# Tying modulation matmuls to the first of their group, and making the first layer's shifts and scales in halves, in a four-layer transformer kernel

## The chip, the cores and the metric

The kernel runs on one core of a Trainium2 chip. The metric is the device time of one execution in microseconds (us), the median of several runs. TensorE does matrix products, VectorE and ScalarE elementwise work (ScalarE also copies and activations), GpSimd a little of it, SyncE (SP) issues the transfers between main memory (HBM) and the on-chip memory. Each engine executes its own queue of instructions in order; semaphores join the queues.

## The reference

256 latent and 256 context tokens of 2048 features go through four blocks: windowed attention with sinks, latent attention (MLA), an RWKV layer with a pooling branch, and full attention. What matters here is the modulation of each block and its use, for two condition vectors (latent and context):

```python
cond = jax.nn.silu(c)[:, None, :]
...
shift, scale, gate = jnp.split(cond @ ada_w[i] + ada_b[i], 3, axis=-1)
h = rmsnorm(x, norm_g[i]) * (1.0 + scale) + shift
...
x = x + gate * o
```

A modulation weight is 2048 by 6144: 2048 columns each for shift, scale and gate. All of it is in 32-bit floating point; the four weights together are 192 MB.

## The kernel before, in words

Feature-major activations `h` lie on chip as two tensors, a high and a low part; each large product is three matmuls (`mm3`, lines 349 to 354: high by high, low by high, high by low), and weights are split on the way in (`split`, lines 314 to 325: a cast on ScalarE at line 323, a difference on VectorE at line 324).

The modulation (`mod_steps`, lines 243 to 281) is a generator that other stages advance step by step, so that its matmuls stand between theirs. The columns are taken in 12 groups of 512: 0 to 3 shift, 4 to 7 scale, 8 to 11 gate. A group's weights come in four loads of 1 MB (`mod_load`, line 240; 192 loads for the four layers), and each load is a group of four matmuls (line 260) that write to four strips of 32 partitions of one PSUM bank, `tile_position=(0, 32 * j)`: the stationary operand has 32 columns only, of which two hold the conditions. When a batch of groups is summed up, ScalarE copies the bank out (line 267), four small matmuls with a selection matrix add the strips up and turn them (line 273), and VectorE adds the bias (line 279). For the first layer a batch is a shift group with its scale group, for the gates and in the other layers four groups.

No order is written out by hand: the program's instructions have priorities in the order in which they are traced, and a scheduler with a model of the engines picks, for each engine, what it thinks ready first. It may put other matmuls between two of one group.

The opening (`tile_network`, from line 1670) loads the activations in four tiles, sums their squares (`add_sq`: squares on ScalarE, lines 1519 and 1522, sums on VectorE, line 1523), makes the reciprocal root and spreads it over the features (lines 464, 456, 474), and then, for each of four blocks `g` of 512 features, waits for the block's shift and scale (`need`), makes the scales (lines 532 and 535) and the four feature tiles of `h` (`put_h`: line 494, cast at 498, difference at 500). Two jobs follow each block, cut into steps: `keys`, the key projection of the block's features (weight tiles `raw`, two feature tiles in each, from two buffers) and `values(g)`, the value projection of the same features into a partial sum `vp` (weight tiles `rawv`, one buffer). Modulation tiles `mraw` have three buffers in the opening. Two modulation loads are issued ahead of the activations, on SP's queue like all others.

Of the kernel before, what the change touches and what calls it, by code (L numbers as in the profile page):

```python
# [13 lines left out]
ALU = mybir.AluOpType  # L14
# [4 lines left out]
P = 128  # L19
D = 2048  # L20
KD = D // P
# [36 lines left out]
VF = 0  # L58
# [12 lines left out]
BKB = 1  # L71


MOD_BATCHES = ((0, 4), (1, 5), (2, 6), (3, 7), (8, 9, 10, 11)), ((0, 4, 1, 5), (2, 6, 3, 7), (8, 9, 10, 11))


_VECS = [
# [39 lines left out]
class Net:  # L117
# [90 lines left out]
    def modulation(self):  # L208
        self.mod = [self.pc.tile([P, 48, 2], F32, name=f"mod{i}") for i in range(4)]
        self.mod_done = set()  # L210
        order = [(i, g) for i in range(4) for gs in MOD_BATCHES[min(i, 1)] for g in gs]
        self.mod_loads = [(i, g, q) for i, g in order for q in range(4)]
        self.mod_ahead, self.mod_pool, self.mod_wait = [], None, 0
        self.side["mod"] = (self.mod_steps(), 0)

# [17 lines left out]
    def mod_load(self):  # L233

        self.mod_wait = 0
        if self.mod_pool and self.mod_loads:
            pool, bufs = self.mod_pool
            raw = pool.tile([P, 4, 512], F32, tag="mraw", name=self.nm("mraw"), bufs=bufs)
            i, g, q = self.mod_loads.pop(0)
            self.nc.sync.dma_start(out=raw, in_=self.I["mod_w"][i, g, q])  # L240
            self.mod_ahead.append(raw)

    def mod_steps(self):
        nc = self.nc
        for i in range(4):
            if i % 2 == 0:
                self.conditions(i // 2)
            mod, cs = self.mod[i], self.cs
            for gs in MOD_BATCHES[min(i, 1)]:
                pb = self.bank("mv")  # L250
                for n, g in enumerate(gs):
                    for q in range(4):
                        while len(self.mod_ahead) < (self.mod_pool[1] - 1 if self.mod_pool and self.mod_loads else 0):
                            self.mod_load()
                        if not self.mod_ahead:
                            self.mod_load()
                        raw = self.mod_ahead.pop(0)
                        for j in range(4):
                            k = 4 * q + j
                            nc.tensor.matmul(  # L260
                                pb[32 * j : 32 * j + 32, :], cs[:, 32 * k + 30 - 2 * n : 32 * k + 62 - 2 * n], raw[:, j, :],
                                start=(n == 0 and q == 0), stop=(n == len(gs) - 1 and q == 3), tile_position=(0, 32 * j),
                            )
                        self.mod_wait = MOD_LAG
                        yield
                ev = self.t512("ev")
                nc.scalar.copy(ev, pb)
                for _ in range(MV_LAG):
                    yield
                p2 = self.bank("mv2")  # L270
                c = 2 * len(gs)
                for j in range(4):
                    nc.tensor.matmul(
                        p2[:, c * j : c * j + c], ev[:, j * P : (j + 1) * P], self.sel[:, :c], start=True, stop=True
                    )
                for n, g in enumerate(gs):
                    bias = self.v("mod_b", i * 48 + g * 4, 4).unsqueeze(2).broadcast_to([P, 4, 2])
                    pv = p2[:, : 4 * c].rearrange("p (j n c) -> p j n c", j=4, c=2)[:, :, n, :]
                    nc.vector.tensor_tensor(mod[:, g * 4 : (g + 1) * 4, :], pv, bias, op=ALU.add)
                    self.mod_done.add((i, g))  # L280
                yield


# [1387 lines left out]
def tile_network(ctx, tc, I, out, dbg=None, stop=9):  # L1671
    N = Net(ctx, tc, I, out, dbg)
    nc = N.nc
# [3 lines left out]
    mod, h = N.mod, N.h  # L1677


    pv = ctx.enter_context(ExitStack())  # L1680
    pV = pv.enter_context(tc.tile_pool(name="v0", bufs=1))
    vh, vl = [pV.tile([P, 4, 512], F32R, name=n) for n in ("vhswa", "vlswa")]
    with tc.tile_pool(name="x0", bufs=1) as px:
        x = [px.tile([P, 4, NT], F32, tag="x0", name=N.nm("x0"), bufs=4) for _ in range(4)]
        acc = px.tile([P, NT], F32, name="acc0")
        N.mod_open(px, 3, 0)
        N.mod_load()
        N.mod_load()
        for k4 in range(0, KD, 4):
            nc.sync.dma_start(out=x[k4 // 4], in_=I["x"][:, k4 : k4 + 4, :])  # L1690
            for k in range(k4, k4 + 4):
                N.add_sq(acc, k, x[k4 // 4][:, k % 4, :])
        pr = N.rms_spread(acc, 4)
        rr = px.tile([P, NT], F32, name="rr0")
        nc.scalar.copy(rr, pr)
        s0 = N.pc.tile([P, KD, 2], F32, name="s0")
        vacc = px.tile([P, 4, 512], F32, name="vacc")

        def keys(kb):

            kb.update({t: N.acc() for t in range(4)})
            for k, wh, wl in N.weights(I["swa_in"][0], KD, 512):
                for t in range(4):
                    s = slice(t * P, (t + 1) * P)
                    N.mm3(kb[t], h[0][:, k, s], h[1][:, k, s], wh, wl, k == 0, k == KD - 1)
                    yield

        def values(g):


            if g < 2:
                whi, wlo = h[0][:, 12:16, :], h[1][:, 12:16, :]
            else:
                whi, wlo = [px.tile([P, 4, 512], F32R, tag="x0", name=N.nm("vw"), bufs=4) for _ in range(2)]
            for q in range(2):
                raw = px.tile([P, 1024], F32, tag="rawv", name=N.nm("rawv"), bufs=RV)
                nc.sync.dma_start(out=raw.rearrange("p (k c) -> p k c", k=2), in_=I["swa_in"][1, 2 * g + q])
                for k in range(2):
                    N.hilo_sb(whi[:, 2 * q + k, :], wlo[:, 2 * q + k, :], raw[:, 512 * k : 512 * k + 512])
            for t in range(4):  # L1720
                s = slice(t * P, (t + 1) * P)
                pb = N.bank("vp")
                for n in range(4):
                    k = 4 * g + n
                    N.mm3(pb, h[0][:, k, s], h[1][:, k, s], whi[:, n, :], wlo[:, n, :], n == 0, n == 3)
                    if n < 3:
                        yield
                if g == 0:
                    nc.scalar.copy(vacc[:, t, :], pb)
                else:  # L1730
                    nc.vector.tensor_tensor(vacc[:, t, :], vacc[:, t, :], pb, op=ALU.add)
                if g == 3:
                    N.hilo_sb(vh[:, t, :], vl[:, t, :], vacc[:, t, :])
                yield

        kb = {}
        kgen = keys(kb)
        todo = []
        for g in range(4):
            owed = 0.0  # L1740
            while len(todo) > VK:
                next(todo.pop(0))
                owed += VR
                while owed >= 1.0:
                    owed -= 1.0
                    if not all((0, i) in N.mod_done for i in (g, 4 + g)):
                        next(N.side["mod"][0])
            N.need(0, (g, 4 + g))
            N.scales(mod[0], N.v("norm_g", 0, KD), s0, 4 * g, 4 * g + 4)
            for k in range(4 * g, 4 * g + 4):  # L1750
                t = N.t512("xr")
                nc.vector.tensor_tensor(t, x[g][:, k % 4, :], rr, op=ALU.mult)
                N.put_h(k, t, s0, mod[0][:, 0:16, :], BOTH)
            todo += [values(g)] * 16 + [kgen] * 16 if VF and g == 3 else [kgen] * 16 + [values(g)] * 16
        owed = 0.0
        while todo:
            next(todo.pop(0))
            owed += VE
            if owed >= 1.0:
                owed -= 1.0  # L1760
                N.advance("mod", 1)
        N.mod_close()
# [3 lines left out]
    with tc.tile_pool(name="x1", bufs=1) as px:  # L1766
# [7 lines left out]
        w = I["swa_out"]  # L1774
# [24 lines left out]
    with tc.tile_pool(name="x2", bufs=1) as px:  # L1799
# [4 lines left out]
        w = I["mla_out"]  # L1804
# [36 lines left out]
    with tc.tile_pool(name="x3", bufs=1) as px:  # L1841
# [4 lines left out]
        gs = N.pc.tile([P, KD, 2], F32, name="gs")  # L1846
# [9 lines left out]
        w = I["ev_out"]  # L1856
# [30 lines left out]
    with tc.tile_pool(name="x4", bufs=1) as px:  # L1887
# [10 lines left out]
        w = I["od_out"]  # L1898
# [39 lines left out]
def layout(inp):  # L1938
    inp = {k: np.asarray(v) for k, v in inp.items()}
    f32 = np.float32  # L1940
    A = {}
# [2 lines left out]
    A["x"] = tok(np.concatenate([ctx, x], axis=0))  # L1944
    A["ctx2"] = tok(inp["ctx_2"][0])
    quads = lambda w: w.reshape(4, 4, P, 12, 512).transpose(3, 0, 2, 1, 4)
    A["mod_w"] = np.ascontiguousarray(np.stack([quads(w) for w in (*inp["ada_w"], *inp["mod_w_2"])]))

    pr, pe = _pairs(P), _pairs(64)
# [10 lines left out]
    w = inp["mla_w_in"][0]  # L1960
# [3 lines left out]
    w = inp["mla_w_qb"][0].reshape(512, 16, 192)  # L1964
    A["mla_qb"] = _tiles(w[:, :, :128].reshape(512, -1), HG * P)
    A["mla_qp"] = _tiles(w[:, :, 128:][:, :, pe].reshape(512, -1), 256)
    w = inp["mla_w_kvb"][0].reshape(256, 16, 256)
# [4 lines left out]
    w = inp["ev_w_in_2"][0]  # L1972
# [22 lines left out]
    for n, g, p in (  # L1995
# [3 lines left out]
        g = inp[g][0][p]  # L1999
# [7 lines left out]
    i = np.arange(P)  # L2007
# [33 lines left out]
```

## Time and profile before

| | |
|---|---|
| median of 3 runs | 3298.6 us (3296.96 to 3299.93) |
| the profiled execution | 3288.34 us, its span 3286.3 us |
| mean granted TensorE clock | 0.983 of full speed |
| TensorE busy (matmuls) | 3117.3 us, 95% of the span, 19762 records |
| VectorE, ScalarE busy | 2101.0 us (64%), 1481.1 us (45%) |
| read from and written to HBM | 517.46 MB, 35.13 MB |

The profile was taken in one execution that was some 10 us shorter than the median of the others. Busy time is a sum over a group of instructions, with overlaps counted once; a matmul's record lasts longer than its spacing to the next, because matmuls are pipelined, so the starts of two records are the safer measure of what one costs. A matmul of the modulation has two records.

### The profile page before, as it was taken

The numbers are of one execution on the slowest core, as the hardware profiler recorded it, in microseconds if no ns is written. First come the engines' busy times: TensorE is split into PE (matmuls) and PEld (weight loads), VectorE is DVE, ScalarE is ACT, GpSimd is POOL, SyncE is SP. The second block draws the span as 40 slices with busy tenths as digits, with TensorE's granted clock in tenths as the row PEclk, the third lists the DMA queues.
The fourth block names the chain that finished last, engine by engine and source line by source line (L and its number), as shares of the span: only waits on it lengthen the run. The fifth ranks groups of instructions, "written<-read, shape, count | busy, mean of one in ns | idle before, by whom it ended". The sixth has DMA issues, their size and how long they took to land. (4 is left out here: it accounts for less than half of the span.)

```text
span 3286.3 us, 53227 instructions
## 1 busy us (share of the span) xinstructions
PE 3117.3 (95%) x19762; PEld 2397.2 (73%) x19762; DVE 2101.0 (64%) x4647; ACT 1481.1 (45%) x3233; POOL 351.2 (11%) x536
## 2 busy tenths in 40 slices
PE   5999999999988999999999999999999999899997
PEld 2567777767777788897776676666677768678897
DVE  2446454553376666666777788777787546857766
ACT  2424444442276666653334334333343323646664
POOL 0000000000001111000122222221121101200000
PEclk8999999999999999999999999999999999999999
DMA  8843444348654666766434433334434474543454
GB/s 303 309 165 135 139 137 157 125 174 290 234 165 142 226 208 226 253 228 211 126 98 133 124 125 116 111 103 149 126 109 154 168 253 130 172 140 129 143 180 153
DMA packets 270771, 556.07 MB, mean 169 GB/s; under 512 B 122928, under 2 KB 150704, under 8 KB 244912
## 3 DMA queue, kind: packets, MB, share of 16 engines
q1 hardware_dynamic: 270512, 552.68, 50.8%
q8 instruction: 155, 2.54, 0.3%
q14 instruction: 104, 0.85, 0.1%
HBM read 517.46 MB, written 35.13 MB: 168 GB/s over the span
## 5 line engine op out<-in xcount | busy, mean ns | idle before, releaser
L324 DVE TENSOR_TENSOR wlo<-raw,whi 128x512 fp32r<-128x512 f32 (+2 forms) x1000 | 660.3, 668 | 572.7 <-ACT whi L323 538.3
L352 PE MATMUL a<-hhi,whi 128*128 128x512 f32 (+1 forms) x2752 | 972.8, 355 | 16.6 <-ACT whi L323 11.9
L323 ACT CAST whi<-raw 128x512 fp32r<-128x512 f32 (+2 forms) x1000 | 593.0, 599 | 815.4 <-PE a L353 470.8
L353 PE MATMUL a<-hlo,whi 128*128 128x512 f32 (+1 forms) x2752 | 947.3, 345 | 0.0
L354 PE MATMUL a<-hhi,wlo 128*128 128x512 f32 (+1 forms) x2752 | 940.0, 347 | 4.5 <-DVE wlo L324 4.3
L352 PEld LDWEIGHTS a<-hhi,whi 128*128 128x128 f32 x2752 | 525.6, 191 | 145.2 <-issue 45.0
L354 PEld LDWEIGHTS a<-hhi,wlo 128*128 128x128 f32 x2752 | 522.6, 191 | 63.5 <-DVE wlo L324 10.2
L353 PEld LDWEIGHTS a<-hlo,whi 128*128 128x128 f32 x2752 | 526.3, 191 | 46.0 <-issue 2.2
L456 POOL TENSOR_TENSOR rs<-st,mhalf 128x4 f32<-128x4 f32 (+3 forms) x109 | 145.7, 1337 | 1683.3 <-DVE st L453 1666.3
L260 PE MATMUL mv<-mraw,cs 128*32 128x512 f32 x1536 | 258.3, 629 | 16.5 <-DMA mraw<-mod_w 16.2
L352 PE MATMUL a<-whi,hhi 128*128 128x512 f32 (+1 forms) x672 | 260.6, 398 | 13.4 <-ACT sq L613 5.9
L353 PE MATMUL a<-wlo,hhi 128*128 128x512 f32 (+1 forms) x672 | 262.7, 391 | 1.4 <-DVE wlo L324 1.1
L354 PE MATMUL a<-whi,hlo 128*128 128x512 f32 (+1 forms) x672 | 258.8, 388 | 0.0
L1427 POOL TENSOR_SCALAR SD<-SV,DL 64x64 f32<-64x64 f32 x224 | 130.0, 580 | 468.7 <-DVE SV L1438 452.4
L352 PEld LDWEIGHTS a<-whi,hhi 128*128 128x128 f32 x672 | 126.1, 190 | 71.2 <-issue 18.6
L353 PEld LDWEIGHTS a<-wlo,hhi 128*128 128x128 f32 x672 | 127.9, 190 | 31.5 <-DVE wlo L324 7.3
L354 PEld LDWEIGHTS a<-whi,hlo 128*128 128x128 f32 x672 | 127.6, 190 | 25.4 <-issue 0.8
L565 ACT ACTIVATE pr<-sc,nm 128x512 f32<-128x512 f32 (+1 forms) x128 | 81.1, 633 | 90.2 <-DVE nm L562 66.7
L1430 ACT COPY SV<-chain 64x64 f32<-64x64 f32 x128 | 26.6, 208 | 184.5 <-DVE SV L1429 178.8
L556 DVE TENSOR_REDUCE mx<-sc 128x1 f32<-128x512 f32 (+1 forms) x128 | 78.9, 617 | 37.8 <-PE sc L766 15.9
L260 PEld LDWEIGHTS mv<-mraw,cs 128*32 128x32 f32 x1536 | 37.0, 110 | 87.8 <-issue 50.3
L1444 ACT COPY y<-chain 64x64 f32<-64x64 f32 x256 | 52.9, 207 | 98.2 <-PE chain L1441 87.8
(379 smaller groups left out, 4690.6 us busy)
## 6 DMA issues: line engine op xcount, KB each, us to landing
mraw<-mod_w SPq DMA_DIRECT2D x192, 1024.0 KB, 4.9
raw<-od_in SPq DMA_DIRECT2D x88, 512.0 KB, 3.6
raw<-swa_in SPq DMA_DIRECT2D x72, 512.0 KB, 3.6
raw<-ev_rkv SPq DMA_DIRECT2D x64, 384.0 KB, 3.4
raw<-ev_in SPq DMA_DIRECT2D x48, 512.0 KB, 3.9
raw<-swa_out SPq DMA_DIRECT2D x40, 512.0 KB, 5.6
raw<-ev_out SPq DMA_DIRECT2D x40, 512.0 KB, 3.6
raw<-mla_g SPq DMA_DIRECT2D x64, 256.0 KB, 3.3
```

The lines of the kernel that those rows point to most:

```text
L260: nc.tensor.matmul(pb[32 * j : 32 * j + 32, :], cs[:, 32 * k + 30 - 2 * n : 32 * k + 62 - 2 * n], raw[:, j, :], start=(n == 0 and q == 0), ...
L323: nc.scalar.copy(whi, raw)
L324: nc.vector.tensor_tensor(wlo, raw, whi.bitcast(F32), op=ALU.subtract)
L352: mm(out, ah, bh, start=first, stop=False, skip_group_check=shared)
L353: mm(out, ah, bl, start=False, stop=False, skip_group_check=shared)
L354: mm(out, al, bh, start=False, stop=last, skip_group_check=shared)
L456: self.nc.gpsimd.tensor_tensor(dst, stv, mv, op=ALU.pow)
L556: nc.vector.reduce_max(mx, sc, axis=AX.X)
L565: nc.scalar.activation(pr[:, :n], sc, AF.Exp, scale=scale, bias=nm, accum_out=sm)
L1427: nc.gpsimd.tensor_scalar(SD[r_], SV[r_, hh, c, :], DL[r_, c : c + 1], None, ALU.mult)
L1430: nc.scalar.copy(SV[half[1], 1, c, :], ps[half[1], P : P + L])
L1444: nc.scalar.copy(y[r_, c, :], blk(3 * P, hh))
```

## The change

The first layer's shift and scale weights get a second layout, `mod_h`: 256 columns to a piece, so that a load of 1 MB holds 8 blocks of 128 rows instead of 4, and a piece takes two loads. A batch is then one half of a shift group with the same half of its scale group, and the opening goes by halves `u` of a block: two feature tiles, half the steps of `keys`, and `values` after the second half. The activations are loaded first, and three modulation loads after them instead of two before. In all layers the matmuls of a load that follow the first one get the highest priority and an edge that keeps them behind the matmul traced before them.

```diff
+MOD_FIRST = tuple(((g, u), (4 + g, u)) for g in range(4) for u in range(2)) + ((8, 9, 10, 11),)
+MOD_BATCHES = (0, 4, 1, 5), (2, 6, 3, 7), (8, 9, 10, 11)
...
     def mod_load(self):
...
-            self.nc.sync.dma_start(out=raw, in_=self.I["mod_w"][i, g, q])
+            if isinstance(g, tuple):
+                raw = raw.rearrange("p k (a c) -> p (k a) c", a=2)
+                self.nc.sync.dma_start(out=raw, in_=self.I["mod_h"][g[0], g[1], q])
+            else:
+                self.nc.sync.dma_start(out=raw, in_=self.I["mod_w"][i, g, q])
...
-            for gs in MOD_BATCHES[min(i, 1)]:
+            for gs in MOD_BATCHES if i else MOD_FIRST:
                 pb = self.bank("mv")
+                half = isinstance(gs[0], tuple)
+                nq, nk, cols = (2, 8, 256) if half else (4, 4, 512)
                 for n, g in enumerate(gs):
-                    for q in range(4):
+                    for q in range(nq):
...
-                        for j in range(4):
-                            k = 4 * q + j
-                            nc.tensor.matmul(
-                                pb[32 * j : 32 * j + 32, :], cs[:, 32 * k + 30 - 2 * n : 32 * k + 62 - 2 * n], raw[:, j, :],
-                                start=(n == 0 and q == 0), stop=(n == len(gs) - 1 and q == 3), tile_position=(0, 32 * j),
-                            )
+
+                        for kk in range(nk):
+                            k, j = nk * q + kk, kk % 4
+                            with self.tc.high_priority(None if kk else 0):
+                                mm = nc.tensor.matmul(
+                                    pb[32 * j : 32 * j + 32, :cols], cs[:, 32 * k + 30 - 2 * n : 32 * k + 62 - 2 * n],
+                                    raw[:, kk, :], start=(n == 0 and k < 4), stop=(n == len(gs) - 1 and k >= KD - 4),
+                                    tile_position=(0, 32 * j),
+                                )
+                                if kk:
+                                    self.tc.keep_in_program_order(mm)
                         self.mod_wait = MOD_LAG
                         yield
-                ev = self.t512("ev")
-                nc.scalar.copy(ev, pb)
+                ev = self.t512("ev", cols=cols)
+                nc.scalar.copy(ev, pb[:, :cols])
...
         N.mod_open(px, 3, 0)
-        N.mod_load()
-        N.mod_load()
         for k4 in range(0, KD, 4):
             nc.sync.dma_start(out=x[k4 // 4], in_=I["x"][:, k4 : k4 + 4, :])
             for k in range(k4, k4 + 4):
                 N.add_sq(acc, k, x[k4 // 4][:, k % 4, :])
+        for _ in range(3):
+            N.mod_load()
...
-        for g in range(4):
+        for g, u in ((g, u) for g in range(4) for u in range(2)):
             owed = 0.0
...
-            N.need(0, (g, 4 + g))
-            N.scales(mod[0], N.v("norm_g", 0, KD), s0, 4 * g, 4 * g + 4)
-            for k in range(4 * g, 4 * g + 4):
+            N.need(0, ((g, u), (4 + g, u)))
+            k0 = 4 * g + 2 * u
+            N.scales(mod[0], N.v("norm_g", 0, KD), s0, k0, k0 + 2)
+            for k in range(k0, k0 + 2):
                 t = N.t512("xr")
                 nc.vector.tensor_tensor(t, x[g][:, k % 4, :], rr, op=ALU.mult)
                 N.put_h(k, t, s0, mod[0][:, 0:16, :], BOTH)
-            todo += [values(g)] * 16 + [kgen] * 16 if VF and g == 3 else [kgen] * 16 + [values(g)] * 16
+            todo += [kgen] * 8
+            if u:
+                todo += [values(g)] * 16
```

What the change moves shows at three places. In these lists a row is one instruction or several alike (`x4`), with its line, its output and inputs and its size; numbers tell buffers apart, and the changed kernel's lines are its own.

TensorE, in the opening, before: the group of the modulation's last load of the first batch (`mv`), the selection matmuls, the next load's group, and the first key matmuls (`a`), whose weights are `whi` and `wlo`.

```order
L260 MATMUL mv_188<-mraw_217,cs_185 32x512 x4
L260 MATMUL mv_188<-mraw_223,cs_185 32x512 x4
L273 MATMUL mv_38_237<-sel,ev_235 128x4 x4
L260 MATMUL mv_293<-mraw_229,cs_185 32x512 x4
L352 MATMUL a_274<-whi_280,hhi 128x512
L353 MATMUL a_274<-wlo_281,hhi 128x512
```

TensorE, in the opening, changed: the groups of loads 7 and 8, with the last keys of the first half between them, the second half's selection matmuls, the groups of loads 9, 10 and 11, and the first key matmul of the second half.

```order
L270 MATMUL mv_269<-mraw_280,cs_187 32x256 x8
L368 MATMUL a_253<-whi_336,hhi 128x512
L369 MATMUL a_253<-wlo_337,hhi 128x512
L370 MATMUL a_253<-whi_336,hlo 128x512
L270 MATMUL mv_269<-mraw_290,cs_187 32x256 x8
L286 MATMUL mv_52_312<-sel,ev_310 128x4 x2
L270 MATMUL mv_346<-mraw_300,cs_187 32x256 x8
L270 MATMUL mv_346<-mraw_347,cs_187 32x256 x8
L270 MATMUL mv_346<-mraw_363,cs_187 32x256 x8
L368 MATMUL a_250<-whi_375,hhi 128x512
```

The first keys stood behind nine loads' groups; now they stand behind five, and those of the second half behind eleven.

SP's queue in the opening, before: modulation loads 16 to 22 (from `mraw_402`) with the second value load of the first block (`rawv_389`) and two key loads (`raw`).

```order
L1717 DMA rawv_389<-swa_in 128x1024
L240 DMA mraw_402<-mod_w 128x2048
L240 DMA mraw_415<-mod_w 128x2048
L240 DMA mraw_496<-mod_w 128x2048
L240 DMA mraw_509<-mod_w 128x2048
L338 DMA raw_515<-swa_in 128x1024
L240 DMA mraw_530<-mod_w 128x2048
L240 DMA mraw_546<-mod_w 128x2048
L240 DMA mraw_561<-mod_w 128x2048
L338 DMA raw_567<-swa_in 128x1024
```

SP's queue in the opening, changed: modulation loads 14 and 15, the same value load (`rawv_435`), and what stands between it and load 16 (`mraw_554`).

```order
L244 DMA mraw_512<-mod_h 128x2048
L244 DMA mraw_529<-mod_h 128x2048
L1733 DMA rawv_435<-swa_in 128x1024
L354 DMA raw_539<-swa_in 128x1024
L354 DMA raw_637<-swa_in 128x1024
L169 DMA row_swa_q<-rows 128x128
L1733 DMA rawv_693<-swa_in 128x1024
L354 DMA raw_803<-swa_in 128x1024
L169 DMA row_swa_qs<-rows 128x128
L169 DMA row_swa_k<-rows 128x128
L244 DMA mraw_554<-mod_h 128x2048
```

Key and value loads stood one by one between modulation loads; now three key loads and a value load stand together in front of load 16.

TensorE in windowed attention, before: transposes of probabilities (`ptr`), a first product with the values (`pv`), and a modulation group in two parts around it.

```order
L591 MATMUL ptr_3125<-ident,pr_2988 128x128
L591 MATMUL ptr_3125<-ident,pr_3007 128x128
L260 MATMUL mv_2769<-mraw_3090,cs_185 32x512
L352 MATMUL pv_2845<-pthi_3115,vhswa 128x256
L260 MATMUL mv_2769<-mraw_3090,cs_185 32x512 x3
L352 MATMUL a_2885<-whi_3182,hhi 128x512
L353 MATMUL pv_2845<-ptlo_3116,vhswa 128x256
```

TensorE in windowed attention, changed: the group of the same load of the first layer's gate.

```order
L607 MATMUL ptr_3406<-ident,pr_3305 128x128
L607 MATMUL ptr_3406<-ident,pr_3323 128x128
L270 MATMUL mv_3096<-mraw_3370,cs_187 32x512 x4
L368 MATMUL pv_3295<-pthi_3411,vhswa 128x256
L368 MATMUL sc_3421<-khswa,qh_1829 128x512
```

All four matmuls now stand between the transposes and the product. Of the 192 loads, 41 had their group broken by other matmuls before (one of them in three parts); none has now.

## Rows read from the trace of the kernel before

**Rows 1.** The page, part 1: busy time, share of the span and records.

```profile
PE 3117.3 (95%) x19762; PEld 2397.2 (73%) x19762; DVE 2101.0 (64%) x4647; ACT 1481.1 (45%) x3233; POOL 351.2 (11%) x536
```

**Rows 2.** Part 5, costliest groups: busy us, mean ns | idle before, releaser.

```profile
L324 DVE TENSOR_TENSOR wlo<-raw,whi 128x512 fp32r<-128x512 f32 (+2 forms) x1000 | 660.3, 668 | 572.7 <-ACT whi L323 538.3
...
L260 PE MATMUL mv<-mraw,cs 128*32 128x512 f32 x1536 | 258.3, 629 | 16.5 <-DMA mraw<-mod_w 16.2
...
L260 PEld LDWEIGHTS mv<-mraw,cs 128*32 128x32 f32 x1536 | 37.0, 110 | 87.8 <-issue 50.3
```

**Rows 3.** Stretches: busy us and records of each engine, granted clock, DMA share.

```profile
0.00:56.00 56.00, 19.51 (x92) 6.39 (x92) 16.09 (x30) 16.08 (x29) 2.19 (x8) 0.87 0.82 316
56.00:60.00 4.00, 3.67 (x9) 2.91 (x10) 2.68 (x4) 3.94 (x8) 0.00 (x0) 0.50 0.82 274
56.00:187.00 131.00, 126.71 (x628) 78.97 (x632) 55.67 (x105) 47.07 (x87) 2.03 (x2) 0.98 0.75 276
300.00:720.00 420.00, 413.69 (x2092) 308.25 (x2091) 223.39 (x566) 194.79 (x431) 13.02 (x12) 1.00 0.40 135
1500.00:2665.00 1165.00, 1120.60 (x7849) 798.61 (x7849) 878.94 (x2025) 441.69 (x1094) 229.76 (x397) 0.99 0.43 133
```

**Rows 4.** Timeline, TensorE in the opening: start us, us, instruction [idle before].

```profile
25.97 1.83 PE L464 MATMUL sums<-ones,acc 128*128 128x2 f32 x8 [25.97 <-DVE acc L1523]
...
30.60 4.69 PE L260 MATMUL mv<-mraw,cs 128*32 128x512 f32 x24
37.35 1.44 PE L260 MATMUL mv<-mraw,cs 128*32 128x512 f32 x8 [2.06 <-DMA mraw<-mod_w]
...
48.89 1.94 PE L260 MATMUL mv<-mraw,cs 128*32 128x512 f32 x8 [2.17 <-DMA mraw<-mod_w]
...
56.33 0.80 PE L352 MATMUL a<-whi,hhi 128*128 128x512 f32 x1 [1.06 <-ACT hhi L498]
```

**Rows 5.** The same view, ScalarE's first squares and SP's next modulation loads.

```profile
12.81 0.63 ACT L1519 ACTIVATE acc<-x 128x512 f32<-128x512 f32 x1 [8.67 <-DMA x<-x]
...
15.30 2.19 ACT L1522 ACTIVATE sq<-x 128x512 f32<-128x512 f32 x4 [0.30 <-DMA x<-x]
...
32.59 37.19 SPq L240 DMA_DIRECT2D mraw<-mod_w  x12
```

**Rows 6.** Timeline, TensorE: one whole group, and two groups in a row.

```profile
214.24 0.39 PE L353 MATMUL a<-wlo,hhi 128*128 128x512 f32 x1
214.47 0.39 PE L354 MATMUL a<-whi,hlo 128*128 128x512 f32 x1
214.78 1.07 PE L260 MATMUL mv<-mraw,cs 128*32 128x512 f32 x8
215.78 0.51 PE L352 MATMUL a<-whi,hhi 128*128 128x512 f32 x1
...
101.89 1.92 PE L260 MATMUL mv<-mraw,cs 128*32 128x512 f32 x16
103.74 0.98 PE L352 MATMUL a<-whi,hhi 128*128 128x512 f32 x3
```

**Rows 7.** Timeline, TensorE in windowed attention: a broken group.

```profile
407.91 1.05 PE L260 MATMUL mv<-mraw,cs 128*32 128x512 f32 x2
408.88 0.39 PE L352 MATMUL pv<-pthi,vhswa 128*128 128x256 f32 x1
409.20 1.06 PE L260 MATMUL mv<-mraw,cs 128*32 128x512 f32 x6
410.19 0.50 PE L352 MATMUL a<-whi,hhi 128*128 128x512 f32 x1
```

**Rows 8.** Timeline, TensorE: the first and the last of 42 lone matmuls.

```profile
244.00 1.04 PE L260 MATMUL mv<-mraw,cs 128*32 128x512 f32 x2
...
2652.85 1.05 PE L260 MATMUL mv<-mraw,cs 128*32 128x512 f32 x2
```

**Rows 9.** Timeline, TensorE: the last value matmul of the opening.

```profile
186.27 0.40 PE L354 MATMUL vp<-vw,hlo 128*128 128x512 f32 x1
```

More of the change, by code (lines that the diff above doesn't have):

```diff
@@ L71 @@
 BKB = 1
-MOD_BATCHES = ((0, 4), (1, 5), (2, 6), (3, 7), (8, 9, 10, 11)), ((0, 4, 1, 5), (2, 6, 3, 7), (8, 9, 10, 11))
+MOD_FIRST = tuple(((g, u), (4 + g, u)) for g in range(4) for u in range(2)) + ((8, 9, 10, 11),)
+MOD_BATCHES = (0, 4, 1, 5), (2, 6, 3, 7), (8, 9, 10, 11)
 _VECS = [
@@ L210, in modulation @@
         self.mod_done = set()
-        order = [(i, g) for i in range(4) for gs in MOD_BATCHES[min(i, 1)] for g in gs]
-        self.mod_loads = [(i, g, q) for i, g in order for q in range(4)]
+        order = [(i, g) for i in range(4) for gs in (MOD_BATCHES if i else MOD_FIRST) for g in gs]
+        self.mod_loads = [(i, g, q) for i, g in order for q in range(2 if isinstance(g, tuple) else 4)]
         self.mod_ahead, self.mod_pool, self.mod_wait = [], None, 0
@@ L270, in mod_steps @@
                 p2 = self.bank("mv2")
-                c = 2 * len(gs)
-                for j in range(4):
+                c, nb = 2 * len(gs), cols // P
+                for j in range(nb):
                     nc.tensor.matmul(
@@ L276, in mod_steps @@
                 for n, g in enumerate(gs):
-                    bias = self.v("mod_b", i * 48 + g * 4, 4).unsqueeze(2).broadcast_to([P, 4, 2])
-                    pv = p2[:, : 4 * c].rearrange("p (j n c) -> p j n c", j=4, c=2)[:, :, n, :]
-                    nc.vector.tensor_tensor(mod[:, g * 4 : (g + 1) * 4, :], pv, bias, op=ALU.add)
+                    o = g[0] * 4 + g[1] * 2 if half else g * 4
+                    bias = self.v("mod_b", i * 48 + o, nb).unsqueeze(2).broadcast_to([P, nb, 2])
+                    pv = p2[:, : nb * c].rearrange("p (j n c) -> p j n c", j=nb, c=2)[:, :, n, :]
+                    nc.vector.tensor_tensor(mod[:, o : o + nb, :], pv, bias, op=ALU.add)
                     self.mod_done.add((i, g))
+                    if half and g[1]:
+                        self.mod_done.add((i, g[0]))
                 yield
@@ L1745, in tile_network @@
                     owed -= 1.0
-                    if not all((0, i) in N.mod_done for i in (g, 4 + g)):
+                    if not all((0, (i, u)) in N.mod_done for i in (g, 4 + g)):
                         next(N.side["mod"][0])
-            N.need(0, (g, 4 + g))
-            N.scales(mod[0], N.v("norm_g", 0, KD), s0, 4 * g, 4 * g + 4)
-            for k in range(4 * g, 4 * g + 4):
+            N.need(0, ((g, u), (4 + g, u)))
+            k0 = 4 * g + 2 * u
+            N.scales(mod[0], N.v("norm_g", 0, KD), s0, k0, k0 + 2)
+            for k in range(k0, k0 + 2):
                 t = N.t512("xr")
@@ L1946, in layout @@
     quads = lambda w: w.reshape(4, 4, P, 12, 512).transpose(3, 0, 2, 1, 4)
+    halves = lambda w: w.reshape(2, 8, P, 24, 256)[:, :, :, :16].transpose(3, 0, 2, 1, 4).reshape(8, 2, 2, P, 8, 256)
+    A["mod_h"] = np.ascontiguousarray(halves(inp["ada_w"][0]))
     A["mod_w"] = np.ascontiguousarray(np.stack([quads(w) for w in (*inp["ada_w"], *inp["mod_w_2"])]))
```

## The prediction

> **What bounds the kernel now.** I read the page's engine line first. TensorE is busy for 95% of the span and VectorE, the next engine, for 64% [rows 1], so time is won where TensorE does less or waits less. The costliest groups then show where the changed code sits: the modulation matmuls of line 260 take 258.3 us of TensorE, and of the 16.5 us that it idles before them 16.2 are waits for their weights [rows 2]. The stretches say where idleness is. In the first 56 us TensorE is busy for 19.51 us; from 56 to 187 us, the rest of the opening, for 126.71 of 131; in the windowed attention (300 to 720 us) for 413.69 of 420; in the RWKV layer (1500 to 2665 us) for 1120.60 of 1165 [rows 3]. So two things can be won: part of the idle start, and TensorE work that is not needed in the full stretches.
>
> The start, in order of time. The activations' first piece is squared at 12.81 us, the second at 15.30: 1 MB lands every 2.5 us [rows 5], and two modulation loads of 1 MB stand ahead of them in SP's queue. The sums start at 25.97, the first modulation group at 30.60. Three loads are there by then; the fourth is issued at 32.59, when the first is used up, and used at 37.35, 4.8 us later; the eighth at 48.89, so four loads took 11.5 us, 2.9 us each [rows 4, 5]. Then come the eviction, the selection matmuls and the first feature tile, and the first key matmul starts at 56.33, 5.5 us after the end (50.83) of the eighth load's group [rows 4].
>
> The second place is a whole group of four modulation matmuls, which fill four strips of the array side by side (8 records; each matmul is two passes). The key matmuls around it start 0.23 us apart. The group starts 0.31 us after the one before it and holds TensorE for 1.00 us until the next one starts; two groups in a row take 1.85 us [rows 6]. In windowed attention a group is broken: one matmul (x2) starts at 407.91 and the next instruction at 408.88, 0.97 us later; the other three (x6) start at 409.20 and hold TensorE until 410.19, 0.99 us [rows 7]. **A lone matmul costs as much as four.**
>
> **The change, part by part.**
>
> *Followers tied.* The program's order, shown with the change, has a broken group become whole. In the program before 41 of the 192 groups are broken, one of them into three; in the trace that is 42 runs of two records, the first at 244.00 and the last at 2652.85 us [rows 8], and 41 longer ones. Whole, a group costs 1.00 us and 0.08 us more than the ordinary spacing in front of it, 1.08 together [rows 6]; broken, 0.97 + 0.99 + 2 x 0.08 = 2.12 [rows 7]. Each of 42 additional pieces thus costs 1.04 us, 43.7 us in all. Where they lie matters: 1 before 300 us, 10 in windowed attention, 3 from 720 to 1500 us, 28 in the RWKV layer (counted by the runs' starts). The first 14 I take in full (14.6 us): attention leaves 6.3 us of 420 idle, so what TensorE doesn't do there is time. The RWKV layer idles 44.4 us of 1165 [rows 3] because it follows a recurrence through other engines; a piece placed in a gap that has to be waited out saves nothing when it goes. I take 70% of its 28 x 1.04 = 29.1 us, nearer the full price since the stretch is 96% busy: 20.4 us. Sum **35 us**, with ends at 0 and 43.7. That a tied group can't be interrupted costs next to nothing: what was allowed in front of a recurrence step before, one matmul, held TensorE for 0.97 us, the group holds it for 1.00.
>
> *Activations ahead of the weights.* Two loads of 2.5 us no longer stand in front, so sums, spread and the first modulation group come 5.0 us sooner, at 25.6 us. SP's queue holds nothing else there.
>
> *First layer in halves.* A load is still 1 MB, but has 8 blocks of 256 columns. The first key tile now waits for 4 loads instead of 8. Three are there; groups start at a slow rate as before (three in 4.69 us [rows 4], 1.6 us each), so the fourth load is issued at about 27.2, used at 32.0 and done at 33.6; 5.5 us later, at 39.1, comes the first key matmul. That is 17.2 us sooner, but it doesn't carry through. The keys of one half are 24 matmuls, and the order shows what follows them: loads 9, 10 and 11 now stand in TensorE's queue in front of the keys of the next half. Seven loads after the fourth at 2.9 us each and two key loads of half a megabyte (1.2 us each) end at 32.0 + 20.3 + 2.4 = 54.7; cast and split add 1.5 (a split is 0.67 us [rows 2], the cast about as long), so the next keys start at about 56.2. At that time the program before is at its first key matmul (56.33) with 9 loads used; the changed one has used 11 and done 24 keys: ahead by 24 x 0.23 + 2 x 1.0 = **7.5 us**. Both then run at the same slow clock, granted at 0.50 from 56 to 60 us [rows 3], and both have some 120 us of TensorE work in front of them, against 28 MB of loads (21 of modulation, 7 of keys and values; 70 to 81 us at 2.5 to 2.9), so the lead stays to the end of the opening. The ends: 0, if the queue of SP gives it all back (below), and 17.2, if loads keep up and the first key matmul's lead carries whole.
>
> *Counted at nothing.* Evictions become 8 of 256 columns instead of 4 of 512 on ScalarE, and the scales and additions of VectorE double to 32 small ones. Both engines are busy for under half of the opening (47.07 and 55.67 us of 131 [rows 3]); without that cover the small operations, some 16 more of 0.2 us, would cost about 3 us. The selection matmuls stay 16. The extra copy of the weights in memory is not read twice.
>
> *Sum.* 35 + 7.5 = 42.5 us. The profiled execution took 3288.3 us (span 3286.3, and 2.0 around it), so it would come to 3245.8; the median of the runs is 3298.6, 10.3 above it, and the forecast in those terms is 3298.6 - 42.5 = **3256 us**.
>
> **The rivals.**
>
> *Pieces were cover.* If the RWKV layer ends with its recurrence, the 28 pieces there only filled gaps, and 14.6 + 7.5 = 22 us are left: 3276.5. For it: 44.4 us idle in spite of filler work. Against it: the next instruction begins 0.97 us after a lone matmul, time after time, so it was ready and waiting.
>
> *The early start carries whole.* 35 + 17.2 = 52 us: 3246.4. For it: DMA engines are only 82% used in the first 56 us [rows 3]. Against it: the three loads in front of the second half's keys.
>
> *Weight loads exposed.* Half-width groups double the weight loads per load of modulation weights. Rows: two groups in a row cost 1.85 us, the second 0.85 [rows 6], so the loads of the second, 110 ns each [rows 2], are hidden under a running pass. A pass of 256 columns lasts half as long, some 0.21 us. If each of the 64 additional passes of 32 loads showed 0.11 us, 7 us go: 3263. The Trainium skill, "TensorE: Matmul & The Clock Gate", Part 3 (The mechanism), says that a weight load overlaps running matmuls only when its row group differs, and strips of columns share all rows; by that rule this rival would be the outcome. The trace of before disagrees at 512 columns, and nothing in it shows 256.
>
> *Slower: SP's queue runs dry.* The order shows that load 16, the last that half 4 needs, now stands behind two key loads, a value load and a third key load, each of which waits for a buffer that TensorE's own progress frees; before, modulation loads stood in between. With three buffers at most three loads are ahead. If for each of halves 4 to 8 TensorE must wait for four fresh loads, 5 x 4 x 2.9 = 58 us are lost in the opening, and even with 35 us from the groups the kernel takes 3298.6 + 58 - 35 = 3322. It decides from 8 us lost at each of the five halves on. Against it: from 54.7 us four modulation loads, two value loads and the split put load 16's issue near 71 us and its arrival near 76; TensorE has 80 matmuls and four loads (22 us) to do from 56.2 on, so it asks near 78.
>
> *Nothing measurable.* The moved rows shift waits elsewhere, and idle time takes the place of the pieces: 3298.6.
>
> **How the numbers follow.** Chances: forecast 0.55 (groups worth 25 to 43.7 us and opening 2 to 14: 3241 to 3272), cover 0.20, early start 0.10, exposed weight loads 0.05, dry queue 0.05, nothing 0.05. The range is 3240 to 3284: both ends of the forecast, the early start, the weight loads and the cover case with an opening worth nothing (14.6 us: 3284). Left out are the dry queue, no change and the edges. A measurement can tell 0.2%, 6.6 us, from no change. Faster by more: 0.55 + 0.20 + 0.10 + 0.05 = 0.90; within: 0.05; slower: 0.05.
>
> **What would show it.** Right: the modulation matmuls' busy time falls from 258.3 to about 215 us; no runs of two records; first group at 25.6 and first key matmul near 39; the last value matmul 6 to 9 us sooner than 186.27 us [rows 9]; the RWKV stretch 15 to 29 us shorter. Wrong: the opening ends no sooner, with waits for modulation weights after 70 us; or runs are whole and the RWKV stretch is as long, with more idle time before the recurrence's matmuls.

## The result and the profile after

| | before | changed |
|---|---|---|
| median of the runs | 3298.2 us (4 runs, 3297.0 to 3299.9) | 3256.3 us (4 runs, 3252.1 to 3270.3) |
| the profiled execution's span | 3286.3 us | 3250.0 us |
| mean granted TensorE clock there | 0.983 | 0.981 |

The ratio is 0.988, 95% interval 0.985 to 0.991: faster. Five more runs of the changed kernel in a later job, beside 23 of the kernel before, gave 3263.8 us (3260.7 to 3267.2) against 3295.8, ratio 0.9909, interval 0.9895 to 0.9922. The gain is thus 32 to 42 us (30 to 40 by the ratios); how far the difference between the two comparisons is explained is a part of what follows.

The page's engine line and the group of modulation matmuls, of the changed kernel:

```profile
PE 3080.6 (95%) x20018; PEld 2399.4 (74%) x20018; DVE 2101.4 (65%) x4663; ACT 1481.1 (46%) x3237; POOL 347.7 (11%) x536
...
L270 PE MATMUL mv<-mraw,cs 128*32 128x512 f32 (+1 forms) x1792 | 212.3, 562 | 16.2 <-DMA mraw<-mod_w 10.9
```

TensorE works 36.7 us less than in [rows 1]: the modulation matmuls fall from 258.3 us [rows 2] to 212.3, although their records grew from 1536 to 1792, and their waits for weights stay at 16 us. No run of two records is left.

Stretches of the changed kernel (us; busy time of TensorE, its weight loads, VectorE, ScalarE, GpSimd; granted clock, DMA share, GB/s). The fourth and the last hold the work of the last two of [rows 3]:

```profile
0.00:56.00 56.00, 26.26 (x208) 15.21 (x212) 18.71 (x37) 19.60 (x36) 1.86 (x8) 0.91 0.80 307
56.00:60.00 4.00, 3.13 (x21) 2.08 (x14) 1.90 (x3) 1.14 (x2) 0.00 (x0) 0.61 1.01 421
56.00:187.00 131.00, 126.17 (x792) 83.51 (x785) 59.11 (x123) 47.80 (x88) 3.03 (x3) 0.95 0.77 281
291.00:702.00 411.00, 403.43 (x2091) 306.06 (x2090) 223.58 (x566) 194.18 (x431) 13.00 (x12) 1.00 0.40 137
...
951.00:996.00 45.00, 34.77 (x145) 22.23 (x143) 22.60 (x66) 18.19 (x47) 5.87 (x9) 0.85 0.61 204
1489.50:2629.00 1139.50, 1094.91 (x7862) 793.70 (x7861) 877.92 (x2027) 441.16 (x1095) 225.52 (x397) 0.98 0.44 136
```

By this execution the opening brought 9 to 11 us, windowed attention 9 (411 for 420), the RWKV layer 25.5 (1139.5 for 1165). From the end of attention to the RWKV layer 7.5 us went back, and about 5 of them at the start of MLA, 45 us here at a granted clock of 0.85, which took 40 us at 0.91 before (from its first `tr<-ident,tw` to the last `tr<-ident,cq` of its start: 971.7 to 1009.6 us before, 957.1 to 999.6 here, 4.6 us more):

```profile
966.00:1006.00 40.00, 31.33 (x130) 20.34 (x132) 21.75 (x65) 17.90 (x48) 4.82 (x8) 0.91 0.53 172
```

TensorE's timeline in the opening of the changed kernel (start, us, instruction, idle before it), to be read against [rows 4] and [rows 9]:

```profile
20.75 1.84 PE L480 MATMUL sums<-ones,acc 128*128 128x2 f32 x8 [20.75 <-DVE acc L1539]
...
25.06 5.00 PE L270 MATMUL mv<-mraw,cs 128*32 128x256 f32 x48
31.68 1.07 PE L270 MATMUL mv<-mraw,cs 128*32 128x256 f32 x16 [1.62 <-DMA mraw<-mod_h]
...
38.18 2.07 PE L368 MATMUL a<-whi,hhi 128*128 128x512 f32 x4 [1.64 <-ACT whi L339]
...
43.17 1.07 PE L270 MATMUL mv<-mraw,cs 128*32 128x256 f32 x16
44.17 0.50 PE L370 MATMUL a<-whi,hlo 128*128 128x512 f32 x1
...
55.81 1.07 PE L270 MATMUL mv<-mraw,cs 128*32 128x256 f32 x16 [2.14 <-DMA mraw<-mod_h]
...
175.55 0.39 PE L370 MATMUL vp<-vw,hlo 128*128 128x512 f32 x1
```

The first group comes 5.5 us sooner than in [rows 4], the first key matmul 18.2, the last value matmul 10.7. Eight matmuls of 256 columns (16 records) hold TensorE from 43.17 to 44.17: 1.00 us, as much as four of 512 [rows 6].

### The profile page after: what moved, and what is told of

It is laid out like the page before. It is cut to its first block, busy times and chain, and to the rows that moved or that the text cites. A ratio compares the mean times of both kernels' runs of the same rounds, so it can differ in the third digit from the quotient of the medians.

```text
span 3250.0 us, 53765 instructions
## 1 busy us (share of the span) xinstructions
PE 3080.6 (95%) x20018; PEld 2399.4 (74%) x20018; DVE 2101.4 (65%) x4663; ACT 1481.1 (46%) x3237; POOL 347.7 (11%) x536
## 5 line engine op out<-in xcount | busy, mean ns | idle before, releaser
L270 PE MATMUL mv<-mraw,cs 128*32 128x512 f32 (+1 forms) x1792 | 212.3, 562 | 16.2 <-DMA mraw<-mod_w 10.9
L1437 DVE COPY Rp<-chain 64x64 f32<-64x64 f32 x256 | 56.7, 221 | 72.1 <-PE chain L1434 69.1
```

The lines of the kernel that those rows point to most:

```text
L270: mm = nc.tensor.matmul(pb[32 * j : 32 * j + 32, :cols], cs[:, 32 * k + 30 - 2 * n : 32 * k + 62 - 2 * n], raw[:, kk, :], start=(n == 0 an ...
L1437: nc.vector.tensor_copy(Rp[half[hh]], blk(0, hh))
```

## Experiments

Two theories were set against each other. The theory of the prediction: each additional piece of a broken group is TensorE work, and it costs time wherever it lies, in the RWKV layer too; the opening adds a few us. The rival: in the RWKV layer pieces were cover for the recurrence, and what is gained comes from the opening and from attention.

**The parts alone: ties, opening, order of loads.** *ties_only* is the kernel before with

```diff
-  nc.tensor.matmul(pb[32 * j : 32 * j + 32, :], ...)
+  with self.tc.high_priority(None if j else 0):
+      mm = nc.tensor.matmul(pb[32 * j : 32 * j + 32, :], ...)
+      if j:
+          self.tc.keep_in_program_order(mm)
```

> The kernel before with the ties alone: no broken group is left (0 additional pieces instead of 42), the opening as before. Theory (each additional piece is about 1.04 us of TensorE and nearly all of it is time): 42 us of the changed kernel less the 9 to 11 that its trace shows at the end of the opening, so 31 to 35 us below before, 3263 to 3267 us, with the RWKV stretch some 26 us shorter. Rival (the pieces of the RWKV layer only filled gaps, and the changed kernel's gain there comes from something else that moved): 14 pieces count, 3283 us.

Measured: 3269.2 us (6 runs, 3260.1 to 3271.1), ratio 0.9904 (0.9886 to 0.9923): 32 us by the ratio, for 42 pieces. That is 2 us above the theory's range and 14 below the rival. The modulation matmuls of its profile:

```profile
L262 PE MATMUL mv<-mraw,cs 128*32 128x512 f32 x1536 | 214.4, 634 | 21.8 <-DMA mraw<-mod_w 21.5
```

The other thing expected, an RWKV stretch some 26 us shorter, isn't in that profile: its recurrence is only 12 us shorter than before (1067 us, below), at a lower granted clock.

*opening_only* is the changed kernel without the ties:

```diff
-  with self.tc.high_priority(None if kk else 0):
+  with self.tc.high_priority(0):
...
-  if kk:
-      self.tc.keep_in_program_order(mm)
```

> The changed kernel without the ties: halves and activations ahead as in it, but its program has 65 additional pieces (4 in the opening, 14 in the rest of the first two layers' loads, 47 later). Theory: 65 x 0.7 to 1.04 us above the changed kernel, 3302 to 3324 us, slower than before in spite of a better opening. Rival (pieces of the later layers are cover): only 18 of them count, 3275 us, faster than before.

Measured: 3306.8 us (12 runs), ratio 1.0028 (1.0017 to 1.0039), in the theory's range and 32 us from the rival: **slower than before**, though its last value matmul comes 8.5 us sooner than in [rows 9]. Halves make the scheduler break more groups: 65 additional pieces in this kernel's order, against 42 before. The modulation matmuls of its profile:

```profile
L270 PE MATMUL mv<-mraw,cs 128*32 128x512 f32 (+1 forms) x1792 | 281.9, 562 | 21.9 <-DMA mraw<-mod_w 15.5 <-DMA mraw<-mod_h 5.7 <-DVE mod L291 0.4
```

That is 69.6 us more busy time than in the changed kernel, 1.07 for each piece. As the mean duration of a record is the same 562 ns, a piece isn't seen in that column; it is seen in the group's busy time, where overlap counts once.

*x_ahead_only* is the kernel before with only the activations moved ahead of its two modulation loads; *x_behind* is the changed kernel with two of its three loads ahead of the activations again:

```diff
         N.mod_open(px, 3, 0)
+        N.mod_load()
+        N.mod_load()
...
-        for _ in range(3):
-            N.mod_load()
```

> The kernel before with the activations loaded ahead and three modulation loads behind them, nothing else; 43 additional pieces instead of 42. Theory: sums and first modulation group 5 us sooner, the fourth load is issued 5 us sooner, so the first key starts at 51 instead of 56.3 us and the time falls by 4 to 5 us, 3294. Rival (the order of the loads is hidden, the first key waits for eight loads whatever comes first): 3298.

Measured: 3294.8 us (12 runs), ratio 0.9992 (0.998 to 1.0003), which tells neither theory from no change. The trace says more: the first key matmul comes 4.7 us sooner (51.6), the last value matmul only 0.6 us.

> The changed kernel with two modulation loads in front of the activations again, as before; halves and ties stay, no additional piece. Theory: the opening ends 4 to 5 us later, 3261 us. Rival (halves alone make the opening's gain, the order of loads is hidden): 3256 us.

Measured: 3267.0 us (6 runs, 3260.9 to 3272.2), ratio 0.9905 (0.9888 to 0.9922), above both theories' figures, which looks like 11 us lost to the order of the loads. The timeline of *x_behind* doesn't show that:

```profile
30.13 4.80 PE L270 MATMUL mv<-mraw,cs 128*32 128x256 f32 x48
...
42.84 0.80 PE L368 MATMUL a<-whi,hhi 128*128 128x512 f32 x1
...
175.49 0.39 PE L370 MATMUL vp<-vw,hlo 128*128 128x512 f32 x1
```

The first group is 5.1 us later than in the changed kernel, the first key 4.7, and the last value matmul stands at the same 175.5: the lead is gone by 60 us. The changed kernel has then begun some 30 key matmuls and used 11 loads, *x_behind* 33 key and 2 value matmuls and 10 loads: what is ahead waits for its weights (2.14 us before the group at 55.81). What *x_behind* loses, it loses later, 8.5 us by the last matmul of the recurrence, of which 1.7 stood at its first; yet from the opening's end on its instructions have the same order as the changed kernel's on all five engines.

**The same program again.** So the changed kernel was run again, unaltered, and beside it a variant with one load ahead and two behind (*x_between*).

> The changed kernel unaltered, beside the next one. From the opening's end on, the kernel with two loads ahead of the activations has the same rows in the same order on every engine, yet it took 3267.0 us against 3256.3 (four runs, one at 3270.3), and in its profile the granted clock was at half level for 54 us of the RWKV layer's chain, against 41 us in the changed kernel's. Theory: the program is the same there and the time at half level differs from run to run, so more runs of the changed kernel spread as those did, median 3256 to 3264 us, some above 3265. Rival: the order of the loads is worth the 11 us; the median stays within 3253 to 3258 us and all runs are below 3262.

Measured: 3263.8 us (5 runs, 3260.7 to 3267.2). The 11 us of *x_behind* fall; no order of loads is told from another. The first comparison's four runs (3252.1, 3254.9, 3257.6, 3270.3) lie lower. By the means it is 5 us, and the time that the clock didn't grant is 5 us less in them (65 against 70), so the clock goes with most of it. What set the clock isn't shown, and chance between executions alone is a poor account: three of the four lie below all 16 runs of this kernel and of the two with another order of loads.

```diff
         N.mod_open(px, 3, 0)
+        N.mod_load()
...
-        for _ in range(3):
+        for _ in range(2):
             N.mod_load()
```

> The changed kernel with one modulation load ahead of the activations and two behind, in place of three behind. All engines keep their order after the opening. Theory (the opening's loads hide each other, the rest is the same program): the first group of modulation matmuls near 27.6 us, the last value matmul at 175.5 us within 1.5, and a median within 6 us of the unaltered changed kernel's in the same job. Rival (each load ahead of the activations costs what it delays): 2.5 us per load at the end of the opening, and half of the 11 us of two loads: 3261 to 3263 us.

Measured: 3265.0 us (5 runs, 3258.5 to 3267.7), 1.2 us from the unaltered kernel, as the theory had it; first group at 27.3, last value matmul at 178.4, where the unaltered kernel of the same job had 177.8. The two last value matmuls are 0.6 us apart, so the theory holds against the 2.5 us per load; the 175.5 that it named was missed by 3 us, by the unaltered kernel too.

What differs between runs of one program shows in the RWKV layer, at the recurrence's outputs. In both profiles of the changed kernel TensorE waits there once for 2.1 us; all its waits in 1800 to 1850 us of the first, then of the second:

```profile
PE yt L1487 <- DVE y L1476: 2.1, 1, 2.1
PE gram L1286 <- DVE AQ L1293: 0.8, 1, 0.8
PE chain L1434 <- ACT y L1460: 0.6, 1, 0.6
PE mv L270 <- DMA mraw<-mod_w: 0.3, 1, 0.3
```

```profile
PE yt L1487 <- DVE y L1476: 2.1, 1, 2.1
PE chain L1434 <- ACT y L1460: 0.6, 1, 0.6
```

And the stretches of 10 us around it, first profile, then second (clock: the third figure from the end):

```profile
1800.00:1810.00 10.00, 9.96 (x104) 6.69 (x104) 4.77 (x13) 3.16 (x10) 0.81 (x4) 1.00 0.50 178
1810.00:1820.00 10.00, 7.85 (x98) 5.21 (x98) 9.75 (x19) 1.12 (x3) 3.40 (x4) 0.91 0.32 105
1820.00:1830.00 10.00, 8.91 (x90) 5.91 (x82) 8.69 (x19) 3.32 (x8) 0.10 (x1) 0.92 0.61 198
1830.00:1840.00 10.00, 9.38 (x55) 6.62 (x53) 8.93 (x22) 3.03 (x11) 2.87 (x5) 1.00 0.70 216
```

```profile
1800.00:1810.00 10.00, 9.96 (x104) 6.63 (x103) 5.17 (x13) 3.16 (x10) 0.29 (x2) 1.00 0.44 154
1810.00:1820.00 10.00, 7.80 (x97) 4.71 (x95) 9.72 (x18) 1.72 (x4) 3.40 (x4) 0.86 0.32 105
1820.00:1830.00 10.00, 10.00 (x74) 6.92 (x70) 7.72 (x16) 2.53 (x6) 0.10 (x1) 0.50 0.53 185
1830.00:1840.00 10.00, 9.43 (x35) 7.12 (x32) 5.23 (x12) 1.45 (x5) 1.18 (x3) 0.50 0.57 151
```

Same work and same longest wait, about 7.8 us busy in the ten that hold it; in one execution the clock drops to its lower level (0.50) for 3.4 us in all, in the other it stays there past 1840, with 74 and 35 records where the first had 90 and 55. Two matmuls of the recurrence (`chain<-SV,AQ`, the same two in both) start 37.2 us apart in the first profile (1795.3 and 1832.5) and 42.5 in the second (1794.7 and 1837.2): 5.3 us lost in one place.

**Where pieces cost.** The kernel before with ties in some layers only:

```diff
-  tied = j > 0
+  tied = j > 0 and i >= 2      # ties_late
+  tied = j > 0 and i < 2       # ties_early
```

> The kernel before with the tie in layers 3 and 4 alone. Its order has 19 additional pieces, 7 in the opening and 12 in the rest of the first two layers (windowed attention above all), none in the RWKV layer. With all groups tied the time was 3269.2. Theory (a piece costs 0.7 to 1.04 us wherever it is): 13 to 20 us more than that, 3282 to 3289 us, of which 3 to 7 us in the opening. Rival (pieces cost only where TensorE has no idle time, so the early ones cost their full 1.04 us and the late ones nothing): 3289 us and the RWKV stretch no shorter than in the kernel before.

Measured: 3282.8 us (12 runs, 3268.0 to 3294.6), ratio 0.9953 (0.9936 to 0.9969): 13.5 us above *ties_only*, 16 by the ratios. The theory's range; and the rival's sign, a stretch no shorter than before, fails below (1055 for 1079 us).

> The kernel before with the tie in the first two layers alone. Its order has 48 additional pieces, none in the first two layers, 10 in the third layer's modulation and 38 behind, most of them in the RWKV layer; the kernel before has 42 in all, 28 of them in the RWKV layer. Theory (a late piece costs as much as any): 3269 + 48 x 0.78 = 3306 us, so no faster than the kernel before (3298), 3299 to 3312. Rival (pieces in the RWKV layer fill gaps of its recurrence and cost nothing): 3269 to 3280 us.

Measured: 3300.3 us (12 runs), ratio 1.0016 (1.0005 to 1.0027): no faster than before, 31 us above *ties_only*, 37 by the ratios, for 48 late pieces. **The rival falls**: 3269 to 3280 was its range.

The recurrence's stretch, from its first matmul to its last, in the profiles of the kernel before (26 lone matmuls in it), *ties_early* (35), *ties_late*, *ties_only*, the changed kernel and its second profile (none each):

```profile
1529.00:2608.00 1079.00, 1040.62 (x7492) 739.47 (x7487) 830.48 (x1940) 412.66 (x1041) 223.51 (x389) 0.99 0.42 128
```

```profile
1530.00:2619.00 1089.00, 1053.63 (x7497) 737.84 (x7496) 833.91 (x1945) 413.46 (x1044) 218.99 (x390) 0.99 0.42 128
```

```profile
1535.00:2590.00 1055.00, 1014.61 (x7499) 734.07 (x7499) 833.19 (x1946) 412.85 (x1044) 219.85 (x390) 0.99 0.43 132
```

```profile
1523.00:2590.00 1067.00, 1028.08 (x7503) 742.96 (x7502) 834.28 (x1947) 413.63 (x1044) 219.86 (x391) 0.97 0.43 130
```

```profile
1516.00:2573.00 1057.00, 1018.00 (x7502) 735.80 (x7500) 831.53 (x1946) 413.01 (x1044) 219.49 (x391) 0.98 0.43 131
```

```profile
1517.00:2579.00 1062.00, 1022.73 (x7501) 739.71 (x7500) 831.74 (x1947) 413.60 (x1044) 219.27 (x391) 0.98 0.43 131
```

At a granted clock of 0.99 the stretch takes 1079 us with 26 lone matmuls and 1055 without: 0.92 us each. *ties_early* and *ties_late*, whose clock there agrees to three digits (0.989, summed over stretches of 5 us; in the kernel before 0.986), lie 34 us apart for 35 pieces. The clock has to be alike in such a comparison: the profile of *ties_late* is the fastest of its 12 runs, and *ties_only*, with no piece either but at 0.97, takes 12 us longer. TensorE's idle time in the stretch is the length less the busy time: 35.4 us with 35 pieces, 38.4 with 26, 38.9 to 40.4 with none. So 5 us at most came back as idle time for 35 pieces, 0.14 us each: as cover the pieces were worth little.

## Why the prediction was right, and where it was off

The time, 3256.3 us, is the forecast's 3256, and its main cause, the pieces, is shown. That the two agree to the us is luck: five later runs of the same kernel give 3263.8, within the forecast's own range, but a gain of 30 to 32 us where the sum has 42.5. Of its terms the pieces came out at 32 us for 35, with what the clock takes back already off, and the opening at 0 to 9 for 7.5. The points:

*Pieces.* A piece adds 1.04 us of TensorE work, as forecast: the modulation matmuls' busy time is 43.9 us lower in *ties_only* (214.4) than in [rows 2], for 42 pieces. In time, the kernels without halves give

| kernel | additional pieces | ratio |
|---|---|---|
| ties_only | 0 | 0.9904 |
| ties_late | 19 | 0.9953 |
| before | 42 | 1 |
| ties_early | 48 | 1.0016 |

0.0112 x 3297 / 48 = 0.77 us a piece, in a line that runs within 2 us of all four. So 42 are worth 32 us, where 35 were forecast. The forecast's split (full price before the RWKV layer, 70% in it) isn't what the runs show: early pieces cost 16 / 19 = 0.85 us, late ones 37 / 48 = 0.77, alike within their intervals, and in the recurrence 0.92 at equal clock. What the 70% stood for, pieces lost in gaps, is small: 0.14 us of idle time a piece in the recurrence, where the forecast took off 0.31. That is some 4 us for the 28 pieces of the RWKV layer; the clock takes some 4 more of the 11 us by which 42 pieces fall short of 1.04 each, and the rest is less than the runs can tell (0.9904 holds within 6 us). A tie also moves other matmuls; that four kernels lie on one line is what puts the time down to the pieces.

*The clock* is the term that the sum lacked. Over the 23 runs of the kernel before in either job the mean granted clock is 0.981; over the nine of the changed kernel 0.979, in *ties_only* 0.979, in *ties_early* 0.983. Time not granted is 1.9% of 3298, 62 us, before, and 68 in the changed kernel: 6 us more. Among runs of the kernel before, a us more of it goes with 0.6 to 0.8 us more time (a line through each set of 23), so some 4 us of the gain are given back. That kernels without late pieces run at a lower mean clock is shown (by the means of their runs five such kernels lie at 0.979 to 0.980, four with them at 0.981 to 0.983); why they do isn't. What went back between attention and the RWKV layer, where the forecast had put 3 us of gain, may belong here in part, which isn't shown: in the four profiles of this program (the changed kernel's two, *x_behind* and *x_between*) the lead shrinks by 4 to 6 us from the end of attention to the first matmul of the recurrence, and the start of MLA ran at 0.85 in place of 0.91.

*The opening.* The steps came within 1.6 us of the forecast: sums at 20.75 (forecast 21.0), first group 25.06 (25.6), fourth load's group 31.68 (32.0), first key 38.18 (39.1), keys of the second half 57.75 (56.2); the last value matmul 10.7 us sooner in one profile and 8.5 in the other (6 to 9). But the order of the loads, which the text counts as 5.0 us in front, adds nothing to the lead at the end: *x_behind* has it too, and *x_ahead_only* has hardly any (0.6 us). The lead comes from the halves. Its worth in the total is less certain: the changed kernel and *ties_only* differ by 1.6 us the wrong way up to 7.9 us the right way, by the ratios of the two comparisons; *x_behind*, whose opening ends as early, stands at 0.9905 in the same job as *ties_only* at 0.9904, and *x_between* at 0.9907. The four profiles with halves and ties lead that of *ties_only* by 10 to 13 us at the last value matmul (188.7 there) and by 3 to 7 at the first matmul of the recurrence. *opening_only*, with 65 pieces, lies 0.0028 x 3297 = 9.2 us above before, where the line of pieces alone would give 23 x 0.77 = 17.7, so its opening is worth 8.5. Between nothing and 9 us; 7.5 was forecast, and the runs don't settle it closer.

*Early start whole* falls: of the first key's 18.2 us, 10.7 are left at the end. *Cover* falls by *ties_early*, but for the 0.14 us above; *Nothing measurable* falls by the ratio's interval, 0.985 to 0.991.

*Weight loads exposed* falls: eight matmuls of 256 columns take 1.00 us with twice the weight loads per column. The rule of the Trainium skill that was cited for it ("TensorE: Matmul & The Clock Gate", Part 3) doesn't describe this case; by it the half-width group would have been the longer one.

*SP's queue runs dry* falls, though its place was sized too kindly. SP in the changed kernel:

```profile
75.61 0.42 SPq L169 DMA_DIRECT2D row_swa_qs<-rows  x1
76.09 0.42 SPq L169 DMA_DIRECT2D row_swa_k<-rows  x1
78.79 14.36 SPq L244 DMA_DIRECT2D mraw<-mod_h  x6
```

Load 16 is issued at 78.79, not near 71, later than TensorE was to ask for it (78). TensorE had other matmuls: from 56 to 187 us it idles 131 - 126.17 = 4.8 us, against 4.3 before, and after 70 us none of it for modulation weights.

## What to carry to other kernels

Here a matmul that fills one strip of the array holds TensorE as long as four side by side (0.97 us against 1.00), so a scheduler that may split such a group breaks it at a full group's price: look in the trace for records that stand alone, and count them before and after every change. A change that moves work, like the halves, can break more groups than it is worth; tie first, then move. Filler work in a stretch that follows a recurrence is only free if TensorE's idle time there grows by as much when it goes: compare length less busy time, in profiles with the same granted clock.

## What the runs showed of the hardware

The same program, with the same longest wait of 2.1 us, runs at the lower level of the clock for 3.4 us in one execution and for 24 us in the next (1817 to 1841 us of the second profile). Runs of one kernel spread by up to 27 us (3268.0 to 3294.6 in *ties_late*, where the mean granted clock goes from 0.984 to 0.975), and the median of four runs of the changed kernel lay 7.5 us below that of five others: one profile, or four runs, can mislead by that much.
